# A two-block transformer kernel: more fill between the inverse products of a scan, priority on VectorE, values of four key blocks at a time, and a merge with its own sum tile, five gate buffers and four banks

## The chip, the cores and the metric

The kernel is one program on one core of a Trainium2 chip. The metric is the device time of one execution in microseconds (us). Lower is better.

The core has five engines that run side by side, each with its instructions in a fixed order: TensorE (PE: matmuls; PEld is its weight loads), VectorE (DVE), ScalarE (ACT), GpSimd (POOL) and SyncE (SP), which issues the DMAs here. An instruction that waits holds up all that stand behind it on its engine.

## The reference

Two blocks run one after the other on a sequence of 2048 tokens with 1024 features. The first projects the normalised tokens, runs two chunked recurrences in both directions (a gated delta rule, whose chunks need the inverse of a unit triangular matrix, and a gated linear attention), and merges the two branches:

```python
sol = lax.linalg.triangular_solve(a_mat + eye, rhs, left_side=True, lower=True, unit_diagonal=True)
...
def merge_branches(o_a, o_b, p, a_norm_l, b_norm_l, w_a_out_l, w_b_out_l, w_out_l):
    y_a = rms_norm_gated(o_a, a_norm_l, p['a_gate']) @ w_a_out_l
    y_b = rms_norm_gated(o_b, b_norm_l, p['b_gate']) @ w_b_out_l
    gates = jax.nn.sigmoid(p['merge'].reshape(*p['merge'].shape[:-1], N_BRANCH, D_MODEL))
    return (gates[..., 0, :] * y_a + gates[..., 1, :] * y_b) @ w_out_l
...
        h_lat = layer_norm(DEEPNORM_ALPHA * h_lat + gate_l * sub_lat) * ln_g[l] + ln_b[l]
```

The second block is a causal attention with 8 heads of value width 64, a gating unit, and an output projection:

```python
        sc = jnp.einsum('bqhd,bkhd->bhqk', qi, k).astype(jnp.float32) * scale
        mask = kpos[None, :] <= qpos[:, None]
        p = jax.nn.softmax(jnp.where(mask[None, None], sc, -jnp.inf), axis=-1).astype(v.dtype)
        return jnp.einsum('bhqk,bkhd->bqhd', p, v)
```

All of it is float32.

## The kernel before

Large products are made of three matmuls each (`mm3`): the operands are split into a high and a low part, and high times high, high times low and low times high are summed (L188, L189, L190).

**The scans** (from 1055 to 2153 us). `weave` (L545) writes PE's order by hand. It interleaves the generators of the two recurrences with a stream of projection matmuls, the *fill* (`d<-uAh,whi` and the like, groups of three matmuls 128x512). It keeps a planned clock: each generator yields its planned cost and a factor, and is not taken up again before the factor times 900 ns (`late`) of plan have passed; until then other generators and fill are taken. The fill's share is fixed (0.91). `gdn_inverse` (from L917) makes the inverses of two chunks at a time. A product on PE (`lv`, L940, two matmuls) is followed by a subtraction on DVE (`R`, L964, L975, L981), whose result is the next product's operand, so a pair is a chain of PE, DVE, PE, DVE. `gdn_scan` takes the inverse `I`, makes `r` (L1022), `pv` (L1026), `vn` (L1028) and the next state `S`. The other engines' orders are made by a scheduler from the data dependences and a priority; `tc.high_priority` moves an instruction forward in it.

**The merge** (from about 2186 to 2690 us) goes over 8 blocks of 256 tokens. `branch` (L1336) loads both scans' outputs and the branch gates of 128 tokens, squares (L1351), reduces (L1354), normalises and gates; `turned` transposes and splits the result into `yh` (ACT, L1367) and `yl` (DVE, L1368). `merge` (L1371) makes, for each of 8 feature tiles m, two products `pp` (with `w_a`, then `w_b`; 12 matmuls 128x256 each), multiplies them by the gates `mg` (L1384), adds both in `mg`'s first half (L1386), and splits that sum into `mh` (ACT) and `ml` (POOL). `mg` is loaded with the raw gates (L1376, buffers of its own, `MGB`), and ACT makes their tanh in it (L1378). `residual` then multiplies by `w_out` (`acc`, 128x512), adds the input `xt` (L1428), normalises in place (ending with L1292) and stores the tile to `d_h` (L1433). `xt` has two buffers; the next load into one (L1420) waits until the store from it has landed. PE's order is the program's order here too: merge of a block, then its residual, with the transposes of the next block in between.

**The attention** (from 3187 to 3802 us). `scores` makes the scores of one key block of 128 keys for 512 queries, ACT their exponentials `pT`. `weigh` (L1845) multiplies `pT` with the block's values, whose 64 columns go to one half of PE's columns by the key block's parity, so the blocks go in pairs. The main loop puts the two `weigh` of a pair into a list, to run `PVL` units later. `gather` (L1850) adds the halves up and makes the reciprocal of the softmax sums, spread over 64 columns (`li`, L1872); `finish` (L1875) brings it to the layout of the outputs with four matmuls and multiplies.

Of the kernel before, what the change touches and what calls it, by code (L numbers as in the profile page):

```python
# [48 lines left out]
PTB = 6  # L49
QB = 5  # L50
PVL = 4
GL = 2
LIP = 0
# [4 lines left out]
MGB = 3  # L58
# [6 lines left out]
VBF = 2  # L65
PRB = 2
# [26 lines left out]
def block_kernel(ctx: ExitStack, tc: tile.TileContext, A, out):  # L93
# [791 lines left out]
    with ExitStack() as gctx:  # L885
        BW = 256
        nch = BW // P
        with tc.tile_pool(name="c1", bufs=2, side="right") as c1, tc.tile_pool(name="c1s", bufs=1, space=PSUM) as c1s, \
# [25 lines left out]
            def gdn_inverse():  # L914
# [32 lines left out]
                for t in range(0, STEPS, 2):  # L947
# [6 lines left out]
                    if d == 0:  # L954
# [3 lines left out]
                        yield 427.0, 1.0  # L958
                        R = X
                        for j in range(3):  # L960
                            lv = sums()
                            times(lv, Yt, R)
                            R = new("R") if j < 2 else new("I")
                            dve.tensor_sub(R, X, lv)  # L964
                            if j < 2:
                                yield 427.0, 1.0
                        I = R
                    else:
# [6 lines left out]
                        dve.tensor_sub(R, one, lv[:, 0:2])  # L975
                        yield 853.0, 1.0
                        for j in range(2):
                            lv = sums()
                            times(lv, Yt, R)
                            R = new("R")  # L980
                            dve.tensor_sub(R, one, lv)  # L981
                            yield 427.0, 1.0
# [7 lines left out]
                    yield 427.0, 1.0  # L990

            def gdn_scan():
# [19 lines left out]
                for t in range(STEPS):  # L1012
# [6 lines left out]
                    if i:  # L1019
                        pa = c1s.tile([P, P], F32, tag="pa", name="pa")  # L1020
                        pe.matmul(out=pa, lhsT=kT, rhs=S, start=True, stop=True)
                        dve.scalar_tensor_tensor(out=r, in0=pa, scalar=c_r[:, d, h, n:n + 1], in1=r, op0=ALU.mult,  # L1022
                                                 op1=ALU.add)
# [6 lines left out]
                    if i < NCH - 1:  # L1030
# [5 lines left out]
                        else:  # L1036
                            dve.scalar_tensor_tensor(out=Sn, in0=S, scalar=eGt[:, d, h, n:n + 1], in1=ps, op0=ALU.mult,
                                                     op1=ALU.add)
# [288 lines left out]
    with ExitStack() as mctx:  # L1327
# [11 lines left out]
        def branch(b, j):  # L1339
# [10 lines left out]
            sq = br.tile([P, KT, P], F32, tag="sq", name="sq")  # L1350
            act.activation(out=sq, in_=o, func=AF.Square)  # L1351
            ss = br.tile([P, KT], F32, tag="ss", name="ss", bufs=2)
            rs = br.tile([P, KT], F32, tag="rs", name="rs", bufs=2)
            dve.tensor_reduce(out=ss, in_=sq, op=ALU.add, axis=AX.X)  # L1354
# [17 lines left out]
        def merge(b):  # L1372
            for m in range(KT):
# [5 lines left out]
                for s in range(2):  # L1379
                    pp = m1s.tile([P, 512], F32, tag="pp", name="pp")[:, 0:256]  # L1380
# [5 lines left out]
                dve.tensor_add(mg[:, 0, :], mg[:, 0, :], mg[:, 1, :])  # L1386
                act.copy(out=mh[:, m, :], in_=mg[:, 0, :])  # L1387
                pool.tensor_tensor(out=ml[:, m, :], in0=mg[:, 0, :], in1=mh[:, m, :].bitcast(F32), op=ALU.subtract)  # L1388

        def turn(t, nr, nw, order, w0, tag):  # L1390

            n = nr * nw
            for s in range(2):
                tp = m1s.tile([P, 4, P], F32, tag=tag, name="tp")
# [53 lines left out]
        m1 = mctx.enter_context(tc.tile_pool(name="m1", bufs=1, side="right"))  # L1448
        mh = m1.tile([P, KT, 256], F32R, name="mh")
# [231 lines left out]
    with ExitStack() as actx:  # L1681
# [119 lines left out]
        LI = (dve, pool)[LIP]  # L1801
# [46 lines left out]
        def gather(h, g):  # L1848
# [3 lines left out]
            if r0_ == 0:  # L1852
                o_[m, g] = (tb.tile([P, GQ], F32, tag=f"o2{g}", name="o2", bufs=1),
                            tb.tile([P, 4, P], F32, tag=f"li{g}", name="li", bufs=1))
# [12 lines left out]
            for j in range(4):  # L1867
# [3 lines left out]
            dve.reciprocal(out=l4, in_=l4)  # L1871
            LI.tensor_tensor(out=li[:, :, rs_], in0=on64.unsqueeze(1).to_broadcast([P, 4, 64]),  # L1872
                              in1=l4.unsqueeze(2).to_broadcast([P, 4, 64]), op=ALU.mult)

        def finish(m, g):  # L1875
# [3 lines left out]
            ps = psa.tile([P, GQ], F32, tag="ms", name="ms", bufs=MSB)  # L1879
            for j in range(4):  # L1880
                pe.matmul(out=ps[:, j * P:(j + 1) * P], lhsT=li[:, j], rhs=ident, start=True, stop=True)
# [89 lines left out]
        with tc.manual_schedule(engines=PE_ONLY):  # L1971
# [11 lines left out]
            on64 = tb.tile([P, 64], F32, name="on64", tag="on64", bufs=1)  # L1983
            pool.memset(on64, 1.0)
# [3 lines left out]
            for u, (n, h, g, kb) in enumerate(units):  # L1988
# [13 lines left out]
                if kb % 2:  # L2002
                    wait += [(u + PVL, weigh, (h, g, k)) for k in (kb - 1, kb)]
                    if h == 3 and g == NG4 - 1:
                        wait += [(u + PVL, value, (1, k)) for k in (kb - 1, kb)]
# [62 lines left out]
```

## Time and profile before

| | us |
|---|---|
| three runs | 3999.57, 3989.38, 3994.24 (median 3994.24) |
| the profiled execution, its own time | 3978.06 |
| its span, first to last instruction | 3976.3 |
| PE busy (share of the span) | 3577.2 (90%) |
| DVE busy | 2481.2 (62%) |
| POOL busy | 1395.6 (35%) |
| ACT busy | 1373.1 (35%) |

The profiled execution is 16.2 us shorter than the median of the runs, and its time is 1.8 us more than its span. Busy time is the time in which an engine executed something; PE's gaps are what an order or a wait can cost or give back.

### The profile page before, as it was taken

What the parts mean: (1) busy time and instruction counts of PE and PEld (TensorE: products, weight loads), DVE (VectorE), ACT (ScalarE), POOL (GpSimd) and SP (SyncE); (2) the same over time, 40 slices, a digit from 0 to 9 for tenths busy, and PEclk for the clock granted to TensorE, in tenths of its full rate; (3) what the DMA queues carried; (4) which work ended last, traced back from release to release, by engine and by line L of the source; (5) the groups of instructions that cost most, each with busy time, mean ns of one, the idle gap of its engine ahead of it and who ended that gap; (6) DMA issues with size and microseconds to landing.
All of it is one profiled execution on the core that took longest, in us unless ns stands there. A gap on an engine that the chain in (4) does not pass through costs nothing.

```text
span 3976.3 us, 57274 instructions
## 1 busy us (share of the span) xinstructions
PE 3577.2 (90%) x18998; PEld 2868.6 (72%) x18998; DVE 2481.2 (62%) x6394; ACT 1373.1 (35%) x3379; POOL 1395.6 (35%) x1666
## 2 busy tenths in 40 slices
PE   4799998888899999988889787878999999999999
PEld 0578877776788887877777677777888765565577
DVE  3645657887776776666665755546405377777766
ACT  0444542221254444444443322212212244444400
POOL 2310124440355555555552311110122246666610
PEclk7899999999999999999999898988999999999999
DMA  5322347763344444544545433324333510001254
GB/s 155 112 61 76 89 139 244 231 183 67 104 135 127 133 130 132 149 136 140 159 142 145 139 103 98 100 88 125 116 103 112 181 47 26 26 18 44 68 170 148
DMA packets 528220, 467.25 MB, mean 118 GB/s; under 512 B 91705, under 2 KB 446371, under 8 KB 527732
## 3 DMA queue, kind: packets, MB, share of 16 engines
q1 hardware_dynamic: 527700, 463.54, 39.3%
q8 instruction: 151, 2.47, 0.3%
q14 instruction: 145, 1.19, 0.1%
q0 software_dynamic: 224, 0.05, 0.0%
HBM read 302.08 MB, written 161.37 MB: 117 GB/s over the span
## 4 chain that ended last, share of the span: by engine, by line
PE 38%; DMA 9%; DVE 8%; issue 4%; ACT 2%; POOL 1%; SPq 0%; DVEq 0%; ACTq 0%; POOLq 0%
PE d L188 4%; PE d L189 4%; PE d L190 4%; PE po L1845 3%; PE acc L188 2%; PE acc L189 2%; PE acc L190 2%; DMA d_h<-xt 2%; PE sx L1782 2%; DMA mg<-d_gate 2%; PE st L1812 2%; PE lv L940 2%; PE st L1813 1%; PE st L1814 1%; DMA o<-d_ob 1%
## 5 line engine op out<-in xcount | busy, mean ns | idle before, releaser
L188 PE MATMUL d<-uBh,whi 128*128 128x512 f32 x832 | 364.2, 438 | 18.3 <-ACT gy L835 13.1
L188 PE MATMUL d<-uAh,whi 128*128 128x512 f32 x832 | 357.9, 430 | 11.6 <-DVE gy L848 6.0
L189 PE MATMUL d<-uAl,whi 128*128 128x512 f32 x832 | 333.9, 401 | 5.8 <-DVE uAl L464 5.8
L189 PE MATMUL d<-uBl,whi 128*128 128x512 f32 x832 | 334.9, 403 | 0.0
L235 POOL TENSOR_TENSOR wlo<-wraw,whi 128x512 fp32r<-128x512 f32 x128 | 168.4, 1316 | 467.9 <-ACT whi L234 442.4
L190 PE MATMUL d<-uAh,wlo 128*128 128x512 f32 x832 | 332.3, 399 | 0.0
L190 PE MATMUL d<-uBh,wlo 128*128 128x512 f32 x832 | 332.3, 399 | 0.0
L1818 ACT ACTIVATE pT<-st 128x512 f32<-128x512 f32 (+1 forms) x320 | 170.0, 532 | 232.2 <-PE st L1814 139.7
L1836 POOL TENSOR_TENSOR acc<-acc,pT 128x512 f32<-128x512 f32 (+1 forms) x168 | 185.9, 1107 | 120.7 <-ACT pT L1818 110.9
L1787 DVE TENSOR_REDUCE mx<-sx 128x1 f32<-128x512 f32 (+3 forms) x288 | 169.4, 616 | 47.5 <-PE sx L1782 29.0
L1388 POOL TENSOR_TENSOR ml<-mg,mh 128x256 fp32r<-128x256 f32 x64 | 57.4, 896 | 395.5 <-ACT mh L1387 305.5
L188 PEld LDWEIGHTS d<-uBh,whi 128*128 128x128 f32 x832 | 161.0, 194 | 43.7 <-ACT gy L835 14.0
L188 PEld LDWEIGHTS d<-uAh,whi 128*128 128x128 f32 x832 | 160.6, 193 | 35.9 <-ACT pre L769 5.1
L190 PEld LDWEIGHTS d<-uBh,wlo 128*128 128x128 f32 x832 | 159.3, 192 | 35.4
L190 PEld LDWEIGHTS d<-uAh,wlo 128*128 128x128 f32 x832 | 159.4, 192 | 33.8
L189 PEld LDWEIGHTS d<-uAl,whi 128*128 128x128 f32 x832 | 160.4, 193 | 26.8 <-DVE uAl L464 6.4
L189 PEld LDWEIGHTS d<-uBl,whi 128*128 128x128 f32 x832 | 161.3, 194 | 20.1 <-DVE uBl L464 0.4
L940 PE MATMUL lv<-R,Yt 128*128 128x128 f32 x576 | 100.2, 298 | 82.1 <-DVE R L975 48.7
L631 DVE SCALAR_TENSOR_TENSOR y<-st,VT,y 128x512 f32<-128x512 f32 (+1 forms) x224 | 165.0, 769 | 4.6
L188 PE MATMUL pp<-yh,w_a_out_h 128*128 128x256 f32 x256 | 84.4, 330 | 91.1 <-DVE mg L1384 89.9
L1845 PE MATMUL po<-pT,v 128*64 128x512 f32 (+3 forms) x640 | 161.0, 562 | 3.3 <-DVE o L1859 3.3
L940 PEld LDWEIGHTS lv<-R,Yt 128*128 128x128 f32 x576 | 81.3, 197 | 110.5 <-DVE R L975 58.2
(593 smaller groups left out, 10620.3 us busy)
## 6 DMA issues: line engine op xcount, KB each, us to landing
wraw<-in_w_in_dram SPq DMA_DIRECT2D x126, 256.0 KB
k<-d_k SPq DMA_DIRECT2D x144, 192.0 KB
d_p<-pre SPq DMA_DIRECT2D x64, 384.0 KB
d_gate<-gy SPq DMA_DIRECT2D x96, 256.0 KB
rows<-d_rows SPq DMA_DIRECT2D x36, 512.0 KB
pr<-d_p SPq DMA_DIRECT2D x128, 128.0 KB
mg<-d_gate SPq DMA_DIRECT2D x64, 256.0 KB
wm<-in_w_mod_dram SPq DMA_DIRECT2D x24, 512.0 KB
```

The source lines that it names most:

```text
L188: pe.matmul(out=out, lhsT=lh, rhs=rh, start=start, stop=False)
L189: pe.matmul(out=out, lhsT=lh, rhs=rl, start=False, stop=False)
L190: pe.matmul(out=out, lhsT=ll, rhs=rh, start=False, stop=stop)
L235: pool.tensor_tensor(out=lo[:, ks, :n], in0=raw[:, :, :n], in1=hi[:, ks, :n].bitcast(F32), op=ALU.subtract)
L631: dve.scalar_tensor_tensor(out=y[:, :w], in0=st[:, o + j:o + j + w], scalar=tap, in1=y[:, :w], op0=ALU.mult, op1=ALU.add)
L940: pe.matmul(out=lv[:, c], lhsT=a[:, c], rhs=b[:, c], start=True, stop=True)
L1782: pe.matmul(out=ps[:, :w], lhsT=qh[0:96, j * P:(j + 1) * P], rhs=kTh[h % 2][0:96, b * 512:b * 512 + w], start=True, stop=not last)
L1787: dve.tensor_reduce(out=m4[:, j:j + 1] if one else mx[:, j, b:b + 1], in_=ps[:, :w], op=ALU.max, axis=AX.X)
L1812: pe.matmul(out=ps[:, c0:], lhsT=kt_h[0:100, ks], rhs=qh[0:100, c0:], start=True, stop=False)
L1818: act.activation(out=pT[:, c0:], in_=ps[:, c0:], func=AF.Exp, scale=SCALE)
L1836: (dve if on_dve else pool).tensor_tensor(out=acc[:, c0:], in0=src[:, c0:], in1=pT[:, c0:], op=ALU.add)
L1845: pe.matmul(out=po_[h, g][r:r + 64, c0:], lhsT=val[kb][:, vs], rhs=pT_.pop((h, g, kb))[:, c0:], start=kb < 2, stop=kb >= 4 * g + 2, skip_g ...
```

## The change

In the scans every factor of `gdn_inverse` goes from 1.0 to 1.7, so a generator comes back after 1530 ns of plan where it was 900. DVE's subtractions `R`, and two operations of `gdn_scan`, get a high priority. In the merge there are five `mg` buffers where there were three, the sum has a tile `ms` of its own, the products `pp` are in a pool of four PSUM banks where they shared two, and eight ACT squares of 128 columns with a running sum replace one square of 1024 and DVE's reduction. In the attention `weigh` runs for four key blocks at a time, `PVL` is 3, `pT` has 8 buffers, and `li` holds one number for each head, which `finish` spreads with a copy.

```diff
--- before.py
+++ after.py
@@ -46,16 +46,15 @@
 POB = 1
-PTB = 6
+PTB = 8
 QB = 5
-PVL = 4
+PVL = 3
 GL = 2
-LIP = 0
 AD = 3
...
 DSP = 0
-MGB = 3
+MGB = 5
 QZB = 2
@@ -63,6 +62,7 @@
 VBF = 2
+SLACK = 1.7
 PRB = 2
@@ -955,15 +955,16 @@
                         act.copy(out=Yt, in_=lv)
-                        yield 427.0, 1.0
+                        yield 427.0, SLACK
                         R = X
...
                             R = new("R") if j < 2 else new("I")
-                            dve.tensor_sub(R, X, lv)
+                            with tc.high_priority(PRI):
+                                dve.tensor_sub(R, X, lv)
                             if j < 2:
-                                yield 427.0, 1.0
+                                yield 427.0, SLACK
                         I = R
@@ -972,14 +973,16 @@
                         R = new("R")
-                        dve.tensor_sub(R, one, lv[:, 0:2])
-                        yield 853.0, 1.0
+                        with tc.high_priority(PRI):
+                            dve.tensor_sub(R, one, lv[:, 0:2])
+                        yield 853.0, SLACK
                         for j in range(2):
...
                             R = new("R")
-                            dve.tensor_sub(R, one, lv)
-                            yield 427.0, 1.0
+                            with tc.high_priority(PRI):
+                                dve.tensor_sub(R, one, lv)
+                            yield 427.0, SLACK
                         lv = sums("lv3")
@@ -987,7 +990,7 @@
                         nxt = load(t + 2)
-                    yield 427.0, 1.0
+                    yield 427.0, SLACK
@@ -1019,8 +1022,9 @@
                         pe.matmul(out=pa, lhsT=kT, rhs=S, start=True, stop=True)
-                        dve.scalar_tensor_tensor(out=r, in0=pa, scalar=c_r[:, d, h, n:n + 1], in1=r, op0=ALU.mult,
-                                                 op1=ALU.add)
+                        with tc.high_priority(PRI):
+                            dve.scalar_tensor_tensor(out=r, in0=pa, scalar=c_r[:, d, h, n:n + 1], in1=r, op0=ALU.mult,
+                                                     op1=ALU.add)
                         yield 213.0, 1.0
@@ -1034,8 +1038,9 @@
                         else:
-                            dve.scalar_tensor_tensor(out=Sn, in0=S, scalar=eGt[:, d, h, n:n + 1], in1=ps, op0=ALU.mult,
-                                                     op1=ALU.add)
+                            with tc.high_priority(PRI):
+                                dve.scalar_tensor_tensor(out=Sn, in0=S, scalar=eGt[:, d, h, n:n + 1], in1=ps,
+                                                         op0=ALU.mult, op1=ALU.add)
                     if n < NT:
@@ -1347,11 +1352,11 @@
             act.activation(out=sg, in_=sg, func=AF.Silu)
-            sq = br.tile([P, KT, P], F32, tag="sq", name="sq")
-            act.activation(out=sq, in_=o, func=AF.Square)
             ss = br.tile([P, KT], F32, tag="ss", name="ss", bufs=2)
             rs = br.tile([P, KT], F32, tag="rs", name="rs", bufs=2)
-            dve.tensor_reduce(out=ss, in_=sq, op=ALU.add, axis=AX.X)
+            for k in range(KT):
+                sq = br.tile([P, P], F32, tag="sq", name="sq", bufs=2)
+                act.activation(out=sq, in_=o[:, k, :], func=AF.Square, accum_out=ss[:, k:k + 1])
             rsqrt(br, ss, rs, 1e-6, "m1r", mul=1.0 / P)
@@ -1377,21 +1382,22 @@
                 for s in range(2):
-                    pp = m1s.tile([P, 512], F32, tag="pp", name="pp")[:, 0:256]
+                    pp = m1p.tile([P, 512], F32, tag="pp", name="pp")[:, 0:256]
                     for k in range(4):
...
                                              op1=ALU.mult)
-                dve.tensor_add(mg[:, 0, :], mg[:, 0, :], mg[:, 1, :])
-                act.copy(out=mh[:, m, :], in_=mg[:, 0, :])
-                pool.tensor_tensor(out=ml[:, m, :], in0=mg[:, 0, :], in1=mh[:, m, :].bitcast(F32), op=ALU.subtract)
+                ms = m1.tile([P, 256], F32, tag="ms", name="ms", bufs=2)
+                dve.tensor_add(ms, mg[:, 0, :], mg[:, 1, :])
+                act.copy(out=mh[:, m, :], in_=ms)
+                pool.tensor_tensor(out=ml[:, m, :], in0=ms, in1=mh[:, m, :].bitcast(F32), op=ALU.subtract)
...
             for s in range(2):
-                tp = m1s.tile([P, 4, P], F32, tag=tag, name="tp")
+                tp = (m1p if tag == "pp" else m1s).tile([P, 4, P], F32, tag=tag, name="tp")
                 for k in range(4):
@@ -1446,6 +1452,7 @@
         m1 = mctx.enter_context(tc.tile_pool(name="m1", bufs=1, side="right"))
+        m1p = mctx.enter_context(tc.tile_pool(name="m1p", bufs=4, space=PSUM))
         mh = m1.tile([P, KT, 256], F32R, name="mh")
@@ -1851,7 +1857,7 @@
                 o_[m, g] = (tb.tile([P, GQ], F32, tag=f"o2{g}", name="o2", bufs=1),
-                            tb.tile([P, 4, P], F32, tag=f"li{g}", name="li", bufs=1))
+                            tb.tile([P, 4, 2], F32, tag=f"li{g}", name="li", bufs=1))
             o2, li = o_[m, g]
@@ -1868,17 +1874,17 @@
             dve.tensor_reduce(out=l4, in_=ps, op=ALU.add, axis=AX.X)
-            dve.reciprocal(out=l4, in_=l4)
-            LI.tensor_tensor(out=li[:, :, rs_], in0=on64.unsqueeze(1).to_broadcast([P, 4, 64]),
-                              in1=l4.unsqueeze(2).to_broadcast([P, 4, 64]), op=ALU.mult)
+            dve.reciprocal(out=li[:, :, h % 2], in_=l4)
...
             ps = psa.tile([P, GQ], F32, tag="ms", name="ms", bufs=MSB)
+            lw = tb.tile([P, 4, 2, 64], F32, tag="lw", name="lw", bufs=1)
+            dve.tensor_copy(out=lw, in_=li.unsqueeze(3).to_broadcast([P, 4, 2, 64]))
             for j in range(4):
-                pe.matmul(out=ps[:, j * P:(j + 1) * P], lhsT=li[:, j], rhs=ident, start=True, stop=True)
+                pe.matmul(out=ps[:, j * P:(j + 1) * P], lhsT=lw[:, j].rearrange("p a b -> p (a b)"), rhs=ident, start=True, stop=True)
             z = tb.tile([P, GQ], F32, tag="z", name="z")
@@ -1999,10 +2003,10 @@
                     value(0, 4 * g + 4 + kb)
-                if kb % 2:
-                    wait += [(u + PVL, weigh, (h, g, k)) for k in (kb - 1, kb)]
+                if kb % 4 == 3:
+                    wait += [(u + PVL, weigh, (h, g, k)) for k in range(kb - 3, kb + 1)]
                     if h == 3 and g == NG4 - 1:
-                        wait += [(u + PVL, value, (1, k)) for k in (kb - 1, kb)]
+                        wait += [(u + PVL, value, (1, k)) for k in range(kb - 3, kb + 1)]
                 if kb == 4 * g + 3:
```

PE's order in the scans is made by the planner. Here is a stretch of the chain of the first pair of chunks of the scans, before (`lv` is the inverse's product, `X`, `R` and `Yt` its operands; `d` the fill; `px` is of the other scan).

```order
L940 MATMUL lv_8512<-X,Yt 128x128 x2
L188 MATMUL d<-uBh,whi 128x512
L189 MATMUL d<-uBl,whi 128x512
L190 MATMUL d<-uBh,wlo 128x512
L188 MATMUL d<-uBh,whi 128x512
L189 MATMUL d<-uBl,whi 128x512
L190 MATMUL d<-uBh,wlo 128x512
L940 MATMUL lv_8523<-R,Yt 128x128 x2
```

And the same place in the changed kernel.

```order
L940 MATMUL lv_8515<-X,Yt 128x128 x2
L188 MATMUL d<-uBh,whi 128x512
L189 MATMUL d<-uBl,whi 128x512
L190 MATMUL d<-uBh,wlo 128x512
L188 MATMUL d<-uBh,whi 128x512
L189 MATMUL d<-uBl,whi 128x512
L190 MATMUL d<-uBh,wlo 128x512
L188 MATMUL d<-uBh,whi 128x512
L189 MATMUL d<-uBl,whi 128x512
L190 MATMUL d<-uBh,wlo 128x512
L940 MATMUL lv_8532<-R,Yt 128x128 x2
```

Between the products of `X` and of the `R` made from it there were two groups of three fill matmuls, and now there are three.

SP's order in the merge, of one block, before (`o` and `sg` are the next block's inputs to `branch`, `mg` the gates, `d_h` the store of a normalised tile, `xt` the residual's input).

```order
L1348 DMA sg<-d_gate 128x8x128
L1376 DMA mg<-d_gate 128x2x256
L1433 DMA d_h<-xt 4x32x1024
L1376 DMA mg<-d_gate 128x2x256
L1420 DMA xt<-in_x_dram 128x1x1024
L1376 DMA mg<-d_gate 128x2x256 x2
L1433 DMA d_h<-xt 4x32x1024
L1376 DMA mg<-d_gate 128x2x256
L1420 DMA xt<-in_x_dram 128x1x1024
L1376 DMA mg<-d_gate 128x2x256 x3
```

And in the changed kernel.

```order
L1353 DMA sg<-d_gate 128x8x128
L1439 DMA d_h<-xt 4x32x1024
L1426 DMA xt<-in_x_dram 128x1x1024
L1381 DMA mg<-d_gate 128x2x256 x3
L1439 DMA d_h<-xt 4x32x1024
L1381 DMA mg<-d_gate 128x2x256 x2
L1426 DMA xt<-in_x_dram 128x1x1024
L1381 DMA mg<-d_gate 128x2x256 x3
```

Before, of a block's eight gates three were issued a block earlier (the last row), one stood ahead of the first store, one between it and the first `xt`, and three behind that `xt`. Now five are issued a block earlier (the two rows behind the second store), and the other three still stand behind the first `xt`, which comes right after the store that it waits for.

ACT's order at the end of a block's residual, before (`yh` is the split of the next block's branch, `sq` the square, `mh` the split of the merged sum).

```order
L1367 CAST yh<-sg 128x4x128 x2
L1351 ACTIVATE sq<-o 128x1024
L1349 ACTIVATE sg<-sg 128x1024
L1367 CAST yh<-sg 128x4x128 x2
L1351 ACTIVATE sq<-o 128x1024
L1349 ACTIVATE sg<-sg 128x1024
L1387 CAST mh<-mg 128x256 x2
L1378 ACTIVATE mg<-mg 128x512
```

And in the changed kernel.

```order
L1372 CAST yh<-sg 128x4x128
L1359 ACTIVATE sq,ss<-o 128x128 x3
L1372 CAST yh<-sg 128x4x128
L1359 ACTIVATE sq,ss<-o 128x128 x5
L1372 CAST yh<-sg 128x4x128
L1354 ACTIVATE sg<-sg 128x1024
L1372 CAST yh<-sg 128x4x128
L1359 ACTIVATE sq,ss<-o 128x128 x8
L1354 ACTIVATE sg<-sg 128x1024
L1393 CAST mh<-ms 128x256
```

The second cast to `yh` now stands behind three squares and the third behind five more, which read another tile's `o`.

## Rows read from the trace of the kernel before

**Rows 1.** The page: busy time, share of the span and instructions of each engine.

```profile
PE 3577.2 (90%) x18998; PEld 2868.6 (72%) x18998; DVE 2481.2 (62%) x6394; ACT 1373.1 (35%) x3379; POOL 1395.6 (35%) x1666
```

**Rows 2.** Windows of the stages; busy us (count) of PE, PEld, DVE, ACT, POOL; PEclk.

```profile
1055.00:2153.00 1098.00, 985.20 (x6288) 859.94 (x6287) 746.23 (x2169) 505.09 (x1609) 576.87 (x845) 0.98 0.48 137
...
2197.00:2690.00 493.00, 404.10 (x2366) 364.36 (x2367) 273.32 (x751) 114.67 (x198) 82.69 (x82) 0.91 0.35 104
...
3187.00:3802.00 615.00, 598.17 (x2896) 365.11 (x2895) 443.40 (x790) 277.81 (x529) 366.57 (x321) 0.98 0.12 37
```

**Rows 3.** Waits of PE, scans: total us, times, longest.

```profile
PE lv L940 <- DVE R L975: 48.7, 30, 6.3
...
PE lv L940 <- DVE R L964: 21.5, 27, 2.4
...
PE lv L940 <- DVE R L981: 11.3, 11, 3.6
```

**Rows 4.** Timeline of the scans: start, us, engine, operation [idle before it <-releaser].

```profile
1711.24 0.39 PE L189 MATMUL d<-uBl,whi 128*128 128x512 f32 x1
...
1711.47 0.40 PE L190 MATMUL d<-uBh,wlo 128*128 128x512 f32 x1
...
1714.48 0.94 DVE L1105 SCALAR_TENSOR_TENSOR x<-x,l 128x256 f32<-128x256 f32 x1
...
1716.48 0.84 PE L940 MATMUL lv<-R,Yt 128*128 128x128 f32 x4 [4.17 <-DVE R L975]
...
1717.55 0.63 PE L189 MATMUL d<-uBl,whi 128*128 128x512 f32 x1
...
1717.98 0.63 PE L190 MATMUL d<-uBh,wlo 128*128 128x512 f32 x1
```

**Rows 5.** Timeline of PE in the merge: first matmuls of products in one block.

```profile
2320.24 0.28 PE L188 MATMUL pp<-yh,w_a_out_h 128*128 128x256 f32 x1
...
2328.74 0.36 PE L188 MATMUL pp<-yh,w_a_out_h 128*128 128x256 f32 x1
...
2331.92 0.28 PE L188 MATMUL pp<-yh,w_a_out_h 128*128 128x256 f32 x1
...
2359.05 0.39 PE L188 MATMUL acc<-w_out_h,mh 128*128 128x512 f32 x1
...
2382.65 0.28 PE L188 MATMUL pp<-yh,w_a_out_h 128*128 128x256 f32 x1
```

**Rows 6.** Waits in the merge's steady part: total us, times, longest.

```profile
PE pp L188 <- DVE mg L1384: 91.8, 33, 10.2
...
ACT mg L1378 <- DMA mg<-d_gate: 226.9, 42, 11.7
```

**Rows 7.** Timeline of ACT, DVE and SP after that block's residual.

```profile
2377.77 1.06 ACT L1351 ACTIVATE sq<-o 128x1024 f32<-128x1024 f32 x1 [3.77 <-DMA o<-d_ob]
...
2390.78 1.28 DVE L1292 SCALAR_TENSOR_TENSOR xt<-xt,ln1rs,lnb 128x1024 f32<-128x1024 f32 x1
...
2393.13 0.56 SPq L1433 DMA_DIRECT2D d_h<-xt  x1
...
2404.22 0.57 SPq L1420 DMA_DIRECT2D xt<-in_x_dram  x1
...
2405.22 0.36 SPq L1376 DMA_DIRECT2D mg<-d_gate  x1
...
2413.73 0.63 ACT L1378 ACTIVATE mg<-mg 128x512 f32<-128x512 f32 x1 [7.93 <-DMA mg<-d_gate]
```

**Rows 8.** The reduction (ns min/median/max), and a square with a sum from another stage.

```profile
L1354 DVE TENSOR_REDUCE ss<-sq x16: 1219/1220/1221, 2163.9 to 2574.6; 128x8 f32<-128x1024 f32 x16
...
251.19 0.27 ACT L646 ACTIVATE sq<-tr 128x128 f32<-128x128 f32 x1
```

**Rows 9.** Timeline of PE, attention: a pair of key blocks, and the last batch (six blocks).

```profile
3500.09 1.08 PE L1845 MATMUL po<-pT,v 128*64 128x512 f32 x4
...
3787.11 2.36 PE L1845 MATMUL po<-pT,v 128*64 128x512 f32 x12
```

More of the change, by code (lines that the diff above doesn't have):

```diff
@@ L1799, in shift @@
                               in1=dmask.unsqueeze(2).to_broadcast([4, 4, P]), op=ALU.mult)
-        LI = (dve, pool)[LIP]
         acc_, po_, pT_, o_ = {}, {}, {}, {}
@@ L1982, in block_kernel @@
             psb = actx.enter_context(tc.tile_pool(name="psb", bufs=2, space=PSUM))
-            on64 = tb.tile([P, 64], F32, name="on64", tag="on64", bufs=1)
-            pool.memset(on64, 1.0)
             for i in range(4):
```

## The prediction

> **What bounds the kernel now.** I read the page first: PE is busy 90% of the span, no other engine above 62% [rows 1]. So PE sets the end, and a change can give back PE's gaps, PE time at the lower clock, or PE work itself. The windows by stage then tell where the three parts of the change find something [rows 2]. In the scans PE is busy 985.20 of 1098 us, so 113 us are idle, at a mean granted clock of 0.98. In the merge it is busy 404.10 of 493, so 89 are idle, at 0.91, which is the worst clock of the three. In the attention 598.17 of 615 are busy: 17 us of gaps at most, and what is to be had there is in the matmuls themselves.
>
> The chain of waits of each stage says who ends PE's gaps. In the scans 81.5 of the 113 us, in 68 waits, are one thing: the inverse's next product on PE waits for DVE's subtraction `R` [rows 3]. [...]
>
> In the merge the waits name the gates: 91.8 us of PE's time wait for L1384, which frees the PSUM bank of a product, and L1384 waits for a tanh, which waits for the gate's load [rows 6]. One block shows the size [rows 5]. It takes 62.4 us (2320.24 to 2382.65). One feature tile takes 3.18 (2328.74 to 2331.92), so eight need 25.4, and the residual takes 23.6 (2359.05 to 2382.65). The other 13.4 us are stalls. Their source stands in [rows 7]: the first tile's LayerNorm ends at 2392.06, 9.4 us into the next block, its store is issued at 2393.13, the `xt` load that waits for that store at 2404.22 (11.1 later), and the gates queued behind it on SP (2405.22) give a tanh at 2413.73.
>
> **The change part by part.** *Scans.* The planner adds one group of three fill matmuls between a product and the next: 3 x 0.23 = 0.69 us. I gave each row of both orders the pitch of its kind; over all products PE's own work between one and the next rises from 1.66 to 2.60 us, 0.94 more, because matmuls of the scans come between too. The number of matmuls and the fill's share don't change, so this costs nothing in itself. Taken one by one in the timeline and each cut by 0.94, the 68 waits keep about 31 of their 81.5 us: **-50**. The upper bound is all of them, -81. Priority moves `R` ahead in DVE's order, but at the example's place the same long operations still stand in front, so I count -5 for it, between 0 and the 31 that are left. Clock: a mean of 0.98 over 1098 us is some 22 us lost, and the long gaps that precede it get shorter; I take a quarter, -5 (between 0 and -22). Against this: a chain that starts later and stretches ends later, and the next pair's masks are made by POOL only after it, so the slack ahead of the next first product falls from some 7 to 3.6 us by my count of PE's work, against 1.7 that POOL needs. It is not used up on the mean, +5 for the places where it is (bounds 0 and 72 pairs x 0.5 = 36). Together **-55**, from -15 to -100.
>
> *Merge.* Of a block's gates m0 to m4 are now loaded before it begins; m5 to m7 still stand behind the first `xt`, and so behind the store. Two things pull them in. DVE's order puts the LayerNorm's last operation ahead of the gates' multiplications, and the two reductions of 1.22 us a block are gone [rows 8], so I put the LayerNorm's end 4 us earlier, at 2388; by the distances of [rows 7] the store is issued at 2388.5, `xt` at 2399.6, and the tanh of m5 comes at some 2409. And four banks let PE do two feature tiles ahead of their gates instead of one. PE's start is later: the second cast to `yh` now stands behind squares that wait for `o` (3.77 us in the row), which I count as 1.5, so m0 starts at 2384. Seven tiles take it to 2406.3; m7 waits for m5's banks till 2410.2 and ends at 2413.4. That is 30.7 us after 2382.65 where 25.4 are work: 5.3 of stall, with rounding 5.5. From the stage's own wait of 91.8 us [rows 6], 8 x 5.5 = 44 stay: **-48**. If the LayerNorm ends no sooner, m7 ends 4 us later: -16. If m5 to m7 come in time, everything goes with the clock behind it: -97. The sum tile `ms` takes `mg`'s buffer free for POOL's part sooner; that is in the early gates. ACT's squares cost 8 x 0.27 = 2.2 us [rows 8] instead of 1.06 [rows 7], 16 times; ACT is busy 114.67 of 493 [rows 2], so they matter only through the order, counted above.
>
> [...]
>
> *Attention.* A pair of key blocks takes 1.08 us, the last batch of six blocks 2.36 [rows 9]. The widths in the batch are 512, 512, 512, 384, 128 and 256, and two blocks run side by side, so its columns are (512 + 512 + 256) x 2 passes, at 0.23 for 512 [rows 4] 1.15 us; the pair's are 0.46. Overhead: 0.62 for one pair, 1.21 for three, so each pair has 0.295 and each batch 0.325, of which 0.16 is the modelled tail of any last matmul (0.39 against 0.23). Joining two pairs saves between 0.165 and 0.325; I take 0.2. There are 160 pairs, so 80 joinings: **-16**, bounds -26 and 0. The 32 multiplications for `li` on DVE become 16 copies; DVE is busy 443.40 of 615 us [rows 2] and PE hardly waits for it: nothing, with a wait of up to 0.5 us at 16 places (+8) if a `finish` meets a busy DVE. `PVL` 3 weighs a batch's last block three units after its scores instead of four; with 320 units in 615 us that is 5.8 us for an exponential that ACT (busy 277.81) has to make, so no wait is counted, and the batch needs 7 of the 8 `pT`.
>
> [...]
>
> Sum: -55 - 48 - 16 = **-119**. The profiled execution took 3978.06 us, 1.8 more than its span and 16.2 less than the median of the runs, 3994.24. I put the change on the median: **3875** (a profile would show a span near 3857).
>
> **The rivals.** *The merge keeps its late gates*: nothing moves the LayerNorm, or `yh` behind the squares costs what was won. For it: SP's queue order, in which the store and the `xt` still stand ahead of m5 to m7. Against it: the two extra banks, which hold regardless. Merge -16, total -87: 3907.
> *The wait in the scans moves*: the next pair's masks come late, or `R` is late by more since DVE (busy 68% of the stage [rows 2]) has the same queue in front. Scans -20, total -84: 3910.
> *Everything goes*: scans -90, merge -85, attention -20: 3800.
> *The batch of four gains nothing*, each block paying the pair's overhead: total -103, 3891.
> *Slower than before*: an `R` set early in DVE's order is an instruction that waits for PE with everything behind it, so that `r`, `S` and the fill's evictions are late and PE waits for these. There are 72 pairs with three subtractions each, 216; from 119 / 216 = 0.55 us lost at each, the gain is gone, and at 0.75 the kernel takes 4037. For it: DVE's 68%. Against it: the subtractions' own inputs come, in the order, not later against DVE's than now.
> *The change moves nothing that binds*, 3990: the gaps named above come back whole elsewhere. Little speaks for this with three independent parts.
>
> **How the numbers follow.** Main case 0.42, no gain in the attention 0.08, late gates 0.18, moved wait 0.12, everything 0.12, slower 0.05, nothing 0.03. A change within 0.3% (12 us) can't be told from none in this kernel. Faster by more has the first five, 0.92; same 0.03; slower 0.05. The range of 80% goes from between the main case and "everything", 3815, past the two late cases to 3930, which leaves about 0.1 on either side.
>
> **What would show it.** Right: in the scans, PE's waits for `R` near 31 us instead of 81.5; in the merge, a block period of some 54 us with PE's wait for the gates at the last two feature tiles only, and a first LayerNorm that ends some 5 us into the next block; in the attention, batches of eight matmuls in about 1.9 us and the stage 16 us shorter. Wrong: waits for POOL's masks or for `r`, `S` and `I` in place of those for `R`; a `d_h` store that lands more than 11 us after its issue; PE standing for `yl` or `yh` at a block's start; a `finish` that waits for its copy.

## The result, and the profile after

The changed kernel takes 3904.41 us (3899.96 to 3907.94, four runs) against 3996.01 of the kernel before (a fourth run, 3997.78, has joined the three of the table), a ratio of 0.9772 with a 95% interval of 0.9755 to 0.9789: 92 us faster, where 119 were forecast. The profiled execution has a span of 3898.3 us, 78 less than the profiled one of before.

The page, with the windows of the stages between the same places of the program, answers to [rows 1] and [rows 2].

```profile
PE 3533.4 (91%) x18998; PEld 2867.3 (74%) x18998; DVE 2441.5 (63%) x6362; ACT 1389.2 (36%) x3619; POOL 1396.1 (36%) x1665
```

```profile
1059.00:2126.00 1067.00, 976.28 (x6286) 856.62 (x6285) 732.18 (x2166) 502.88 (x1609) 574.47 (x845) 0.99 0.49 140
2174.00:2621.00 447.00, 379.51 (x2328) 344.11 (x2328) 254.42 (x735) 128.08 (x377) 80.06 (x82) 0.91 0.38 113
3120.00:3724.00 604.00, 577.52 (x2895) 378.69 (x2896) 442.28 (x775) 276.03 (x530) 372.69 (x320) 0.99 0.12 37
```

The scans are 31 us shorter (1098 to 1067), with 22 of it in PE's gaps and 9 in its busy time. The attention is 11 shorter, all of it and more in busy time. From the first product of the merge to the last matmul of its residuals it was 523.6 us and is now 473.2, so 50 less; from there to the first scores of the attention it is 6 more. 31 + 50 + 11 - 6 is 86; the other 8 of the difference to 78 lie in two places. The scans begin 4 us later; in the profiles of all versions below they begin anywhere from 1052.7 to 1059.1, with nothing changed ahead of them. And from the last product of the scans to the first of the merge it is 37.4 us where it was 33.4; the run of the squares alone comes back to this.

PE's waits in the scans answer to [rows 3].

```profile
PE lv L940 <- DVE R L977: 30.8, 21, 4.6
PE pv L1030 <- DVE r L1026: 26.9, 29, 3.9
PE pS L1036 <- ACT vn L1032: 8.7, 17, 1.6
...
PE lv L940 <- DVE R L965: 2.3, 5, 1.0
PE lv L940 <- DVE R L984: 0.8, 1, 0.8
```

The waits for the three subtractions fell from 81.5 us to 33.9; the forecast was 31. But the wait of `pv` for `r` is 26.9, where the kernel before had 4.9:

```profile
PE pv L1026 <- DVE r L1022: 4.9, 6, 2.1
```

One block of the merge, on PE, answers to [rows 5]; then ACT's and SP's rows around it, as in [rows 7], and the row of DVE that says what was late.

```profile
2345.21 0.28 PE L188 MATMUL pp<-yh,w_a_out_h 128*128 128x256 f32 x1
...
2373.27 0.58 PE L188 MATMUL pp<-yh,w_b_out_h 128*128 128x256 f32 x1 [8.03 <-DVE mg L1389]
...
2379.63 0.39 PE L188 MATMUL acc<-w_out_h,mh 128*128 128x512 f32 x1
...
2403.38 0.28 PE L188 MATMUL pp<-yh,w_a_out_h 128*128 128x256 f32 x1
```

```profile
2349.68 0.57 SPq L1439 DMA_DIRECT2D d_h<-xt  x1
2359.96 0.57 SPq L1426 DMA_DIRECT2D xt<-in_x_dram  x1
2360.62 1.48 SPq L1381 DMA_DIRECT2D mg<-d_gate  x3
```

```profile
2370.19 0.63 ACT L1383 ACTIVATE mg<-mg 128x512 f32<-128x512 f32 x1 [15.94 <-DMA mg<-d_gate]
```

```profile
2371.95 0.93 DVE L1392 TENSOR_TENSOR ms<-mg 128x256 f32<-128x256 f32 x1 [9.91 <-POOL ml L1394]
```

The block takes 58.2 us where it took 62.4. One stall of 8.03 us is left where the block of [rows 5] had two, ahead of m5 and m6 (the eight feature tiles are m0 to m7):

```profile
2342.99 0.58 PE L188 MATMUL pp<-yh,w_a_out_h 128*128 128x256 f32 x1 [4.66 <-DVE mg L1384]
...
2351.70 0.51 PE L188 MATMUL pp<-yh,w_a_out_h 128*128 128x256 f32 x1 [3.22 <-DVE mg L1384]
```

The one that is left starts at the second product of m6, not at m7. The chain back from it: the store is issued 4.5 us into the block, `xt` 10.3 later, the gate of m5 gets its tanh at 2370.19; the splits of earlier sums stand behind that tanh on ACT, POOL waits for them, and DVE can write no third `ms`. The wait as a whole in the steady part is 57.7 us (91.8 before, [rows 6]):

```profile
ACT mg L1383 <- DMA mg<-d_gate: 177.9, 28, 16.1
DVE ms L1392 <- POOL ml L1394: 70.0, 8, 10.1
...
PE pp L188 <- DVE mg L1389: 57.7, 9, 8.2
```

In the attention, four key blocks take 1.87 us from their first matmul to the next instruction:

```profile
3405.70 1.94 PE L1851 MATMUL po<-pT,v 128*64 128x512 f32 x8
3407.57 0.39 PE L188 MATMUL ms<-wkvh,kvh 128*128 128x256 f32 x1
```

### The profile page after: what moved, and what is told of

Read it like the earlier page. It is cut to its first block, busy times and chain, and to the rows that moved or that the text cites. A ratio compares the mean times of both kernels' runs of the same rounds, so it can differ in the third digit from the quotient of the medians.

```text
span 3898.3 us, 57395 instructions
## 1 busy us (share of the span) xinstructions
PE 3533.4 (91%) x18998; PEld 2867.3 (74%) x18998; DVE 2441.5 (63%) x6362; ACT 1389.2 (36%) x3619; POOL 1396.1 (36%) x1665
## 4 chain that ended last, share of the span: by engine, by line
PE 51%; DVE 17%; issue 11%; DMA 11%; POOL 4%; ACT 3%; SPq 2%; DVEq 0%; POOLq 0%; ACTq 0%
PE d L188 7%; PE d L189 7%; PE d L190 7%; PE po L1851 3%; DVE Mt L818 3%; PE acc L190 2%; PE acc L188 2%; PE acc L189 2%; PE lv L940 2%; PE sx L1789 2%; DMA wraw<-in_w_in_dram 2%; DVE M L820 2%; PE st L1818 2%; DMA rows<-d_rows 1%; PE st L1820 1%
## 5 line engine op out<-in xcount | busy, mean ns | idle before, releaser
L1394 POOL TENSOR_TENSOR ml<-ms,mh 128x256 fp32r<-128x256 f32 x64 | 54.0, 851 | 354.5 <-ACT mh L1393 354.5
L234 ACT CAST whi<-wraw 128x512 fp32r<-128x512 f32 x128 | 78.3, 611 | 213.9 <-DMA wraw<-in_w_in_dram 168.5
L1851 PE MATMUL po<-pT,v 128*64 128x512 f32 (+3 forms) x640 | 143.1, 547 | 0.0
L818 DVE TENSOR_TENSOR Mt<-M 128x1 f32<-128x1 f32 (+40 forms) x155 | 134.2, 866 | 4.0
L1327 POOL TENSOR_TENSOR lo<-raw,hi 128x512 fp32r<-128x512 f32 (+1 forms) x40 | 49.6, 1250 | 233.1 <-ACT hi L1326 230.0
```

What stands on the lines that cost most here:

```text
L234: act.copy(out=hi[:, ks, :n], in_=raw[:, :, :n])
L818: dve.tensor_tensor(out=t, in0=M[:w, i:i + 1, i + 1:32].to_broadcast([w, L, L]), in1=M[:w, i + 1:32, i + 1:32].rearrange("p j c -> p c j") ...
L1851: pe.matmul(out=po_[h, g][r:r + 64, c0:], lhsT=val[kb][:, vs], rhs=pT_.pop((h, g, kb))[:, c0:], start=kb < 2, stop=kb >= 4 * g + 2, skip_g ...
```

## The experiments

All ratios below are to the kernel before, run beside the experiment on the same chip, where it took 3979 to 3980 us. The whole change has 0.9772, beside 3996 us, so ratios and profiles are compared, not times. The two don't quite agree on the whole change: its ratio says 91 us at 3980, its profile 78. A difference between an experiment and the whole change is therefore known to some 13 us only. The five gate buffers and the sum tile `ms` were not run alone, nor was the whole change without its squares.

**The scans' part alone**: the factor 1.7 and the priorities, as in the diff of the change.

> Only the scans' part of the change (factor 1.7 and the priorities), merge and attention as before. The stages of the two profiles put the scans at -31 us, the merge at -50 and the attention at -11. If the parts are independent, this run takes about 3965 us against 3996 of before, with PE waiting about 34 us for R and 27 us for r. If a shorter scan only shifts a loss into the next stage, it takes 3980 or more.

0.9921 (0.9903 to 0.9940), 31 us. The waits are those of the whole change (R 33, r 25.7), so this part gains alone what it gains in the whole.

**The factor alone**, at every timed yield of `gdn_inverse`; one of them:

```diff
-                        yield 427.0, 1.0
+                        yield 427.0, SLACK
```

> Only the factor 1.7, with no priority. Theory P (the priorities make the new wait for r, by letting other work settle in front of it on VectorE): PE's wait for R falls to 35 to 45 us, the wait for r stays near the 5 us of before, and the scans gain 45 us, about 3950. Theory S (the longer distance makes it, since the other recurrence's long VectorE operations now fall where r is due): the wait for r is 20 us or more without any priority, and the scans gain 25 us or less, about 3970.

0.9922 (0.9904 to 0.9941). Its waits of PE:

```profile
PE pv L1027 <- DVE r L1023: 27.9, 29, 3.3
PE lv L941 <- DVE R L976: 27.3, 19, 4.4
```

The wait for `r` is there without any priority, so theory S holds in its mechanism; the gain is 31 us rather than 25 or less.

**The priorities alone** (`SLACK = 1.0`).

> Only the priorities, with the factor at 1.0. Theory P: the wait for r rises from 5 to 20 us or more while the wait for R falls little from 81 (to 70 or above), so the time is 3996 to 4010. Theory S: the wait for r stays near 5, the wait for R falls by 5 to 15, time 3980 to 3992.

0.9991 (0.9979 to 1.0004): no change that can be told from none. The waits for R are 48.7 + 21.1 + 11.0 = 80.8 us and for r 5.0, as before. Theory P is out, and theory S's small gain isn't there either. Alone the priorities gain nothing that shows, and with the factor they add nothing to it (0.9921 with, 0.9922 without).

**The merge's part alone.**

> Only the merge's part (five gate buffers, own sum tile, four banks, eight squares), scans and attention as before. If the parts are independent: a block period of 58 us where it was 63, about 3946 us. If the merge's gain came from the state that the scans leave behind: 3970 or more.

0.9892 (0.9873 to 0.9912), 43 us; the block period is 58 us. From first product to last residual matmul its profile has 477 us (523.6 before), and 7.7 us come back behind it, much as in the whole change (6.4): at the end of the merge PE's transposes wait for the last tiles' LayerNorm, 5.5 us in one wait before and 12.1 in two here.

```profile
PE tp L1396 <- DVE xt L1292: 5.5, 1, 5.5
```

```profile
PE tp L1397 <- DVE xt L1292: 12.1, 2, 6.4
```

**The attention's part alone.**

> Only the attention's part (four key blocks at a time, the copy in finish), scans and merge as before. If a batch of four saves 0.2 us against two pairs: 80 joinings, the stage 11 to 16 us shorter, a ratio to before of 0.9965. If a batch pays at each block what a pair pays: no change, 1.000. What the three parts alone lack to the whole change's 0.977 would then be in the parts together: the scans alone gave 0.992 and the merge alone 0.989, so the product with 0.9965 is 0.978.

0.9979 (0.9967 to 0.9992), 8 us: between the two. The product of the three parts' ratios is 0.9793, beside 0.9772 (0.9755 to 0.9789) for the whole change; within their intervals the parts add up. All the matmuls of `weigh` together, from each batch's start to the next instruction, take 150.4 us before (157 pairs, a median of 1.009, and the batch of six) and 138.9 here (80 batches, a median of 1.867). A joining saves 2 x 1.009 - 1.867 = 0.151 us, 80 of them 12.1. But PE's gaps in the stage rise from 16.8 to 26.1 us: the waits for the maxima (`mx` and `m`) from 8.6 to 13.3, and waits for `acc` (2.9), for `l` (2.2) and for `pT` (2.1) are new, while those for `o` (3.3) and `li` (1.9) are gone. So the batch pays less than a pair at each block, and part of the gain goes to gaps.

**Three tiles `ms` instead of two.**

```diff
-                ms = m1.tile([P, 256], F32, tag="ms", name="ms", bufs=2)
+                ms = m1.tile([P, 256], F32, tag="ms", name="ms", bufs=3)
```

> The whole change with three tiles ms instead of two. Theory M (the 8 us stall at m6 in each block is made by the two ms: the split of the first sums stands on ScalarE behind the tanh of m5, which waits for its late gate, GpSimd then frees no ms, VectorE can add no third sum, and the banks fill up): the sums go one feature tile further, the stall shrinks by 2 to 4 us in seven blocks, 15 to 28 us less than the whole change, a ratio to before of 0.970 to 0.973. Theory G (the banks wait for the gate itself): same as the whole change, 0.977.

0.9801 (0.9771 to 0.9831). The stall moved on by one product, to m7, and little of it went; in the six middle blocks it is 6.1 to 8.6 us, and the stage has 474 us (473 in the whole change), so no gain can be told:

```profile
2369.13 0.58 PE L188 MATMUL pp<-yh,w_a_out_h 128*128 128x256 f32 x1 [6.14 <-DVE mg L1389]
```

Theory G: PE waits for the gate itself. The two `ms` decide only where it stands.

**The store in four pieces**, nothing else.

```diff
-                sp.dma_start(out=hv[4 * i:4 * i + 4], in_=xt)
+                for w in range(4):
+                    sp.dma_start(out=hv[4 * i + w], in_=xt[32 * w:32 * w + 32])
```

> The whole change with each store of a normalised tile (4 x 32 x 1024) issued as four stores of 32 x 1024. Theory Q (the gates m5 to m7 are late because xt waits some 10 us for a store that runs over few DMA engines): the distance from the store to xt falls from 10 to 5 us or less, the stall at m6 falls from 8 to 3 us or less, and the kernel gains 35 us on the whole change, ratio 0.968. Theory L (the landing takes its 10 us however it is cut): the stall stays and the ratio stays at 0.977, or is a little worse for three more issues.

0.9638 (0.9614 to 0.9663): 53 us less than the whole change by the ratios, 55 by the spans of the profiles (3843.6 against 3898.3), all of it in the merge (418.6 us against 473.2), and more than the 35 expected. SP's rows for one block:

```profile
2338.85 1.73 SPq L1440 DMA_DIRECT2D d_h<-xt  x4
2342.78 0.57 SPq L1426 DMA_DIRECT2D xt<-in_x_dram  x1
2343.46 3.91 SPq L1381 DMA_DIRECT2D mg<-d_gate  x3
```

From store to `xt` it is 3.93 us (10.28 in the whole change), and the tanh of m5 comes 20 us into the block instead of 25. The stalls at m6 of the six blocks between the first and the last are 0 to 3.2 us (6.6 to 8.2 in the whole change) and their period is 49 to 52 us. Two windows, one in a store of the whole change and one in a store of four pieces, show what differs; the last three columns are PEclk, the DMA engines' mean busy share and GB/s.

```profile
2351.00:2359.50 8.50, 8.50 (x73) 8.50 (x72) 8.50 (x40) 1.99 (x6) 1.41 (x1) 1.00 0.23 63
```

```profile
2339.50:2342.50 3.00, 3.00 (x28) 3.00 (x27) 2.78 (x9) 3.00 (x17) 0.00 (x0) 1.00 0.76 220
```

With the single store the mean busy share of the 16 DMA engines is 0.23, with the four together 0.76, though a load has a part in that (135 of the window's 660 KB). The store's own packets take 8.7 us from first to last as one and 2.5 as four. Theory Q holds in what was measured: the distance, the stall and the gain. On how many engines a store runs no row shows, only the mean share.

**The factor also between `pa` and `pv`.**

```diff
-                        yield 213.0, 1.0
+                        yield 213.0, SLACK
                     pv = c1s.tile([P, P], F32, tag="pa", name="pv")
```

> The whole change, with the factor 1.7 in the delta-rule scan as well, between the product pa and pv. Theory D (the new wait for r is a distance too short on PE: 1.8 us, unchanged by the change): the wait for r falls from 27 us to under 8 and the scans gain 15 to 20 us, ratio 0.973. Theory B (VectorE is behind by a backlog that some wait has to pay): the waits move on to S, vn or R, their sum stays within 8 us, and the ratio stays at 0.977.

0.9706 (0.9686 to 0.9725): 26 us less than the whole change by the ratios, 39 by the spans, and nearly all of it in the scans. PE's waits there:

```profile
PE lv L940 <- DVE R L977: 13.3, 13, 1.7
PE pS L1036 <- ACT vn L1032: 9.0, 21, 1.2
PE pa L1024 <- DVE S L1042: 8.8, 9, 2.5
PE pv L1030 <- DVE r L1026: 8.4, 12, 1.9
```

Theory D is nearly met in `r` (8.4, against "under 8"), with more gain than its 15 to 20, and theory B is out: the sum doesn't stay, for PE's gaps in the scans fall from 90.7 to 57.9 us. That R's wait halves too was expected by neither.

**Both together.**

> The whole change with both of the edits that gained: the store in four pieces and the factor 1.7 between pa and pv. They lie in different stages. If they add up, the ratio to before is 0.964 x 0.971 / 0.977 = 0.958, some 3810 us against 3980. If the merge's gain needs the scans as they were, 0.962 or more.

0.9549 (0.9533 to 0.9566), 3798.11 us against 3978.57: they add up (0.9638 x 0.9706 / 0.9772 is 0.957). This version beats both kernels: 0.9549 / 0.9772 = 0.977 of the changed one.

**The factor at `vn` as well**, on top of that.

```diff
                     act.copy(out=vn, in_=pv)
-                    yield 213.0, 1.0
+                    yield 213.0, SLACK
```

> The same with the factor 1.7 also between pv and the product pS, which waits for vn (21 waits, 9 us with the factor at pa alone). Theory D (each wait goes where its distance grows): vn's wait falls to 3 us or less and the scans gain 5 us or more, ratio 0.956. Theory C (the delta-rule scan is one chain of 144 steps, which by now is as long as its fill): the waits for vn fall, but the scans get longer or stay, ratio 0.958 or more.

0.9688 (0.9671 to 0.9704), 59 us slower than without. The product `pS`'s wait for `vn` falls from 8.8 to 4.3 us, and that of `pa` for `S` rises from 10.1:

```profile
PE pa L1024 <- DVE S L1042: 60.1, 43, 4.5
```

PE's timeline shows the last fill matmul and the last of the scans:

```profile
2113.03 0.40 PE L190 MATMUL d<-uAh,wlo 128*128 128x512 f32 x1
...
2150.15 0.49 PE L1047 MATMUL po<-vn,pr 128*128 128x128 f32 x2 [0.19 <-ACT vn L1032]
```

The fill is used up 37 us before the scan ends; in the whole change it lasts 31 us longer than the scans. There it bridges PE's way to the first product of the merge. Here PE then stands, as the stretch behind the scans shows, without this edit and with it (us, then busy us and count of PE, PEld, DVE, ACT, POOL; PEclk, DMA share, GB/s):

```profile
2089.00:2127.00 38.00, 26.64 (x113) 20.97 (x111) 13.19 (x42) 17.52 (x63) 2.58 (x2) 0.87 0.55 155
```

```profile
2151.00:2190.00 39.00, 4.21 (x17) 3.42 (x17) 18.18 (x42) 18.31 (x65) 7.15 (x5) 0.53 0.71 203
```

This is theory C in its result: the scan's chain is longer than its fill. Why the wait for `S` grows was not tested by itself. PE's own work between `pS` and the next `pa` has shrunk, from a median of 2.27 us to 1.89, so a factor at `S` might have moved the wait once more.

**Four banks alone** on the kernel before; the transposes that share the tag `pp` move into the same pool.

```diff
-                    pp = m1s.tile([P, 512], F32, tag="pp", name="pp")[:, 0:256]
+                    pp = m1p.tile([P, 512], F32, tag="pp", name="pp")[:, 0:256]
```

> Kernel before with the products pp in four banks and nothing else. If the banks carry the merge's gain (two feature tiles ahead of the gates instead of one): the stalls at m4 and m5, 9 us together in a block, become one of 5 to 6, 3 us a block, 25 us, ratio 0.994. If three gate buffers bind in their place: the block period stays within 1 us of 63, ratio 1.000.

0.9961 (0.9946 to 0.9976), 16 us. That is between the two cases, and neither describes it: the two stalls of before are there with about their length, one tile later (behind m5 and m6, most of them 3 to 5 us); what is gone is the wait of some 2 us behind m0. One block's:

```profile
2521.27 0.58 PE L188 MATMUL pp<-yh,w_a_out_h 128*128 128x256 f32 x1 [4.58 <-DVE mg L1384]
...
2530.17 0.58 PE L188 MATMUL pp<-yh,w_a_out_h 128*128 128x256 f32 x1 [4.20 <-DVE mg L1384]
```

The products of a block take 36.4 us on the mean of the six middle blocks (39.7 before), the residual up to the next block's first product 25.3 (23.6). The banks alone are about a third of the merge's gain.

**The eight squares alone** on the kernel before.

```diff
-            sq = br.tile([P, KT, P], F32, tag="sq", name="sq")
-            act.activation(out=sq, in_=o, func=AF.Square)
...
-            dve.tensor_reduce(out=ss, in_=sq, op=ALU.add, axis=AX.X)
+            for k in range(KT):
+                sq = br.tile([P, P], F32, tag="sq", name="sq", bufs=2)
+                act.activation(out=sq, in_=o[:, k, :], func=AF.Square, accum_out=ss[:, k:k + 1])
```

> Kernel before with the eight squares in place of one square and the reduction, and nothing else. If the squares bring the LayerNorm and the store forward by what the reductions took (1.2 to 2.4 us a block): 10 to 20 us less, ratio 0.996. If yh behind the squares costs as much as that: 1.000. If it costs more: 1.003.

1.0118 (1.0103 to 1.0133): 47 us slower, more than any case allowed for. SP's rows, and what PE waits for in that block:

```profile
2409.86 0.54 SPq L1433 DMA_DIRECT2D d_h<-xt  x1
2420.07 0.57 SPq L1420 DMA_DIRECT2D xt<-in_x_dram  x1
2421.05 12.82 SPq L1376 DMA_DIRECT2D mg<-d_gate  x3
```

```profile
2431.81 0.58 PE L188 MATMUL pp<-yh,w_a_out_h 128*128 128x256 f32 x1 [10.91 <-DVE mg L1384]
```

It isn't ACT's time: eight squares with the reading of their sums take 2.45 us in the changed kernel (2406.51 to 2408.96). With the squares the scheduler makes another order on SP: the store and the `xt` that waits for it now stand next to each other, and gates that were issued ahead of `xt` (in the kernel before, one gate ahead of the store and one between) stand behind it. So PE stands behind m3 for 9 to 11 us in each block but the first, and the stage is 39 us longer (563.0 against 523.6). Reading the cause from the rows is not the same as putting the old order back, which no run did. The squares do bring the store forward, as forecast: it is issued 4.1 us into the block, where it was 10.5. The whole change has the same order on SP, but there m3 and m4 have buffers and are loaded a block earlier, so PE doesn't stand behind m3. What the order costs it at m6 no run shows.

The squares have a second price, outside the stage: from the last product of the scans to the first of the merge it is 37.0 us here, and 36.3 to 37.7 in every version with the squares whose fill lasts; without them it is 33.1 to 34.5.

## Why the prediction was right, and where its sizes were off

The direction, the range and the three parts came as forecast; the time is 29 us above the forecast of 3875, still inside 3815 to 3930.

**Scans, -55 forecast, -31 measured.** The step on the waits for R was right (31 us forecast to be left, 33.9 measured). The step that failed is that nothing else waits in their place: I put +5 on late masks and left `r` at its 5 us. The distance from `pa` to `pv` on PE is not touched by the change (a median of 1.73 us of PE work before, 1.79 after); what filled it was PE's standing for R, which let DVE catch up. With that gone, `r` is behind the same long DVE operations of the other recurrence. That the wait for `r` comes from the factor and not from the priorities is shown by the run of the factor alone, and that its distance sets it by the run with the factor at `pa`, where the median is 2.33. The catching up as the reason is argued from the timelines, not measured by itself. The -5 for the priorities, taken at the wait of [rows 4], was nothing that shows. The -5 for the clock no run shows by itself: the mean granted clock of the scans is 0.99 where it was 0.98. Behind the wait of [rows 4] the trace of before has a granted clock of 0.50 (1718 to 1720 us), and the fill matmuls are 0.43 us apart there where they are 0.23 ahead of the wait.

**Merge, -48 forecast, -50 measured in the stage, -43 by the run of this part alone.** The size was right, but not all of its steps, so that the sum fits so well is in part luck. The store came earlier than I put it (4.5 us into the block, 5.9 forecast), and the tanh of m5 at 25 us (26.4 forecast). I had PE wait 4 us at m7; it waited 8 at m6, since I counted the PSUM banks and not the two `ms`; with three it waits at m7, and still 6 us or more. The products of the six blocks in the middle gave 5.4 us each where I had 6 by the sum and 8 by the block's period; those of the first and the last gave 10.7 each, of which 6.8 went again ahead of the second block, and 4 more came at the last residual. And 6 us came back behind the merge, where the last LayerNorm is now exposed, and 4 ahead of it, as in all versions with the squares; no term had these. That gates late behind `xt` are what is left is shown by the store in four pieces. The banks alone hold 16 of the merge's 43 us; how the rest divides between the five buffers, `ms` and the squares no run shows.

**Squares.** I priced them through ACT's order at 1.5 us a block. Alone they cost 47 us, by the trace through SP's order. The rows of the order showed store and `xt` side by side; I didn't ask which edit made it. That the reductions' end brings the LayerNorm and the store forward was right: with the squares alone the store comes 6.4 us sooner in its block, where I had 4.6. In the whole change the five gate buffers cover m3 and m4.

**Attention, -16 forecast, -8 alone, -11 in the whole change.** The term of a joining was mis-sized, 0.2 us for a measured 0.151 (my lower bound from the rows was 0.165). I had put a pass of two blocks side by side at the fill's 0.23 us; in the trace of before the two start 7 ns apart, and the next two 0.48 us later (3500.09 and 3500.57). And gaps that I counted as nothing grew by 9 us. 12 less 9 is 3, but the stage's profile has 6 less alone and 11 in the whole change: the matmuls of `gather` take some 4 us less, and the rest is spread over others. No term had that.

**The rivals.** The wait that moves was right in kind and wrong in place (`r`, neither masks nor R), though `r` stood among the signs of being wrong. The late gates are real, but they took little of the forecast gain. The rival that a batch of four gains nothing is out, by 0.151 us at each joining.

## What to carry to other kernels

A wait that ends a chain can hide the next one (here PE's wait for `R` fell from 81.5 to 33.9 us, and that for `r` rose from 4.9 to 26.9): after cutting it, look at what the same late engine feeds next, and give that its distance too, but watch that the chain does not outlast its fill (here it did by 37 us, and the kernel was 59 us slower). A load that waits for a store's landing holds everything behind it on its queue (here `xt` stood 10.28 us behind the store's issue, with three gates behind it), so try the store in pieces before adding buffers (in four it was 3.93 us, with a mean DMA share of 0.76 instead of 0.23, and the kernel took 53 us less). A small edit on one engine can change the order on another (the eight squares on ACT changed SP's, and alone cost 47 us): compare the orders of all queues, also for edits that look free.

## What the runs showed of the hardware that I had not expected

The same 512 KB store took 10.3 us until the load that waits for it was issued when it was one DMA of 4 x 32 x 1024, and 3.9 us when it was four of 32 x 1024; from its first packet to the last it was 8.7 and 2.5 us, and the DMA engines' mean busy share 0.23 and, with some of a load, 0.76.

A square of 128 columns with its sum is two instructions on ACT, 0.29 us and 0.19 for reading the sum; eight took 2.45 us (2406.51 to 2408.96 in the changed kernel), where I had counted 8 x 0.27 = 2.2.
